# PEER layer: the expert activations of 64 tokens from gathered rows of u, the up products on 320 columns

## Chip, cores and metric

The kernel runs on one core of one Trainium2 chip. The metric is the device time of one execution in microseconds (us). The core has a matrix engine (PE, with its weight loads shown apart as PEld), a vector engine (DVE), a scalar engine (ACT), a general engine (POOL) and a queue engine (SP) that only issues DMAs; ACT and POOL issue DMAs too.

## What is computed

Two transformer blocks on 512 tokens of width 1024. The change lies in the last layer, a feed-forward layer that picks experts by product keys (PEER):

```
s = einsum('thpc,hpnc->thpn', q, subkeys)          # 8 heads, 2 halves, 128 keys each
s_top, i_top = top_k(s, 16)                        # of each half
best, pos = top_k(all 16 x 16 sums, 16)            # per head, so 128 experts per token
gates = softmax(best)
act = gelu(einsum('cd,ced->ce', xb, u[eb])) * gates
y = einsum('ce,ced->cd', act, v[eb])
```

There are 16,384 experts, as 128 blocks j of 128. u and v have one row of 1024 numbers per expert. After it come the residual sum and a last norm.

## The kernel before

Everything is float32; a product of two float32 matrices is made as three products of split halves (function mm3, line 192), each 128x128 weights against up to 512 columns.

In the layer (function peer) the tokens are treated in two ways. For tokens 0 to 127 the chosen rows of u and v are gathered, one expert slot k at a time: a row of uv (8 KB, u beside v) per token by an indirect DMA on POOL (gather, line 1421), a dot with the token's row on DVE (line 1429) and a weighted sum (line 1438). For tokens 128 to 511 nothing is gathered. The activations of all experts are computed as dense products: for each block j, `up(j)` runs 8 chunks x 3 products with 384 columns (TD = 384, one per token). They are multiplied by a sparse gate matrix and go through `down`, 18 products of 512 columns per block with v.

The gate matrix comes from one-hot products. `route(t)` finds experts and gates of the 128 tokens of group t on DVE (top-16 searches, index arithmetic, three large one-hot steps per half). `transposed` brings them to columns. `onehots(t)` works in 32 steps of 4 tokens (here called quads): DVE or POOL build the one-hots oh1 (of the row key) and oh2 (of the column key, scaled by the gate), PE multiplies them (line 1344), ACT copies the 128x512 result into `stage` (line 1346). For t = 1 and 2 `stage` is written to DRAM (`Gd`, line 1356) and read back block by block later; for t = 3 it stays on the chip.

While DVE works on that, PE is given `fill`s: up products of the first NA = 42 blocks, made ahead (`up_store`), their gelu stored in DRAM (`Hd`). Weights of u and v come through SP's queue (`pump`, line 110, 512 KB each), ACT makes the high half (line 115), and POOL or DVE the low half (line 118), as the list `lsplit` says. There are three buffers for loaded tiles and three pairs for split ones in this part.

So the layer has two parts. In the first one, routing, one-hots and 42 fills, in the order: 6 fills, route 1, one-hots 1 (with 6 fills), write of Gd with 8 fills, route 2, one-hots 2, and so on. In the second one the 128 blocks run in the order `mix`: a block whose up is not yet made makes it (`gate`), the others read it back, then `down`; the 128 gathers of tokens 0 to 127 run beside it. A list scheduler orders each engine's instructions by the dependences; the engines then run them strictly in that order.

Of the kernel before, what the change touches and what calls it, by code (L numbers as in the profile page):

```python
# [26 lines left out]
NA = 42  # L27
FIRST, FLUSH = 6, (2, 2, 2, 2)
# [15 lines left out]
def body(tc, A, out, upto=None, dbg=None):  # L44
# [1109 lines left out]
    def peer(norm):  # L1154
        H, L = norm.h, norm.l
        TD = 384
# [8 lines left out]
        Hd = dram.tile([NA, P, TD], F32, name="Hd")  # L1165
        keep = ctx.enter_context(tc.tile_pool(name="keep", bufs=1, reuse_waits="tile"))
        xnh = keep.tile([P, 8, TD], F32R, name="xnh")
        xnl = keep.tile([P, 8, TD], F32R, name="xnl")
# [27 lines left out]
        for i in range(16):  # L1196
# [15 lines left out]
            if 0 < i < 9:  # L1212
                c = i - 1
                xf = axps()[:, :TD]
                V.scalar_tensor_tensor(xf, xT[:, c, P:], vec("ffn_norm2", c), norm.rstd[:, P:],
# [23 lines left out]
        def up_store(j):  # L1239
            ps = mmps()[:, :TD]  # L1240
            up(j, ps)
            g = hp.tile([P, TD], F32, name="gel", tag="gel", bufs=3)
            SC.activation(g, ps, AF.Gelu)
            nc.scalar.dma_start(Hd[j], g)
# [8 lines left out]
        def route(t):  # L1253
# [8 lines left out]
            for i0, n, w, o in ((0, 1, 16, 0), (1, 2, 8, 16), (3, 5, 4, 32), (8, 8, 1, 52)):  # L1262
# [4 lines left out]
                                .to_broadcast([P, 8, n, w]), ALU.add)  # L1267
            for h in range(8):
                top16(bv[:, h], bi[:, h], cd[:, h])
            pf = r_("pf", (P, 8, 16))  # L1270
            V.tensor_copy(pf, bi)
            fi, fj, w_ = (r_(n, (P, 8, 16)) for n in ("fi", "fj", "fw"))
            for n, (sh, off) in enumerate(((3, -1.0), (2, -5.0))):
# [5 lines left out]
                else:  # L1279
                    V.scalar_tensor_tensor(fi, w_, off, fi, op0=ALU.add, op1=ALU.max)  # L1280
            V.scalar_tensor_tensor(fi, pf, -44.0, fi, op0=ALU.add, op1=ALU.max)
            V.scalar_tensor_tensor(fj, fi, -16.0, pf, op0=ALU.mult, op1=ALU.add)
            for m, off in ((-8.0, -8.0), (-4.0, -20.0), (-1.0, -44.0)):
                V.scalar_tensor_tensor(w_, fi, m, pf, op0=ALU.mult, op1=ALU.add)
                V.scalar_tensor_tensor(fj, w_, off, fj, op0=ALU.add, op1=ALU.max)
            ev = []
            for half in range(2):
# [3 lines left out]
                                iotap.rearrange("p (o i) -> p o i", o=1).to_broadcast([P, P, 16]), ALU.is_equal)  # L1291
                o4 = oh.rearrange("p (h k) i -> p h k i", k=16)
                V.tensor_tensor(o4, o4, tf[:, :, half].rearrange("p h (o i) -> p h o i", o=1)
                                .to_broadcast([P, 8, 16, 16]), ALU.mult)
                e = r_(f"e{half}", (P, P), bufs=2)
                V.tensor_reduce(e, oh, axis=AX.X, op=ALU.add)
                ev.append(e)
            gt = gate0 if t == 0 else r_("gt", (P, P), bufs=2)
# [7 lines left out]
            return ev[0], ev[1], gt  # L1306
# [3 lines left out]
        def transposed(t):  # L1310
            pt = axps()
            for n, a in enumerate(route(t)):
                PE.transpose(pt[:, n * P:(n + 1) * P], a, ident)
            rt = b_("rt", (P, 3, P), bufs=3)
# [3 lines left out]
        def onehots(t, rt):  # L1318
            io4 = iotp.rearrange("p (o i) -> p o i", o=1).to_broadcast([P, 4, P])
            stage = [stp.tile([P, 64, P], F32, name="stage", tag="stage", bufs=2) for _ in range(2)]  # L1320
            for q4 in range(32):
                t4 = slice(4 * q4, 4 * q4 + 4)
# [4 lines left out]
                if q4 % 3 == 1:  # L1327
# [22 lines left out]
            if t == 3:  # L1350
                return stage
# [340 lines left out]
```

## Time and profile before

| | us |
|---|---|
| median of 3 runs | 2962.44 |
| lowest, highest | 2959.42, 2965.99 |
| the profiled execution, its own time | 2960.28 |
| its span | 2957.9 |
| PE busy | 2900.9 (98%) |
| DVE busy | 1929.8 (65%) |
| ACT busy | 1376.7 (47%) |
| POOL busy | 1158.4 (39%) |

The span runs from the first instruction to the last; the execution's own time holds 2.4 us around it. Busy PE is counted from a matmul's start to its modelled end, and matmuls overlap, so the distance from start to start tells what one costs. The layer's products with u begin at 1750 us of the span.

### The profile page before, as it was taken

The page shows a single profiled execution, that of the slowest core. Times are in us where ns is not written, and L with a number is a line of the kernel's source. Part 1 is how long each engine was busy: PE and PEld are TensorE (multiplying, and loading weights), DVE is VectorE, ACT ScalarE, POOL GpSimd, SP SyncE. Part 2 cuts the span into 40 slices and gives each one's busy share as a digit, 9 for nine tenths or more (in the row PEclk, how much of TensorE's full clock was granted, in tenths as well). Part 3 has the DMA queues.
Part 4 walks back from the last instruction along what each step waited for, and adds up shares of the span by engine and source line. Part 5 has one row for each costly group of instructions (what it writes and reads, how often), then busy time and mean ns, then how long its engine had stood idle before and what let it go on. Part 6 is the DMA issues. An engine that isn't in the chain of part 4 may idle for free.

```text
span 2957.9 us, 46911 instructions
## 1 busy us (share of the span) xinstructions
PE 2900.9 (98%) x18211; PEld 2619.5 (89%) x18211; DVE 1929.8 (65%) x3505; ACT 1376.7 (47%) x2346; POOL 1158.4 (39%) x749
## 2 busy tenths in 40 slices
PE   8999999999999999999999999889999999999998
PEld 8999999988899999776688888888889888888887
DVE  4556645567664646537655788888677776776676
ACT  4454433356542425434544447567444444444444
POOL 4224323342232424104421435446455554555453
PEclk9999999999999999999999999999999999999999
DMA  4112333331123223221142232773888888888885
GB/s 136 67 52 101 98 96 101 97 104 36 65 97 97 96 98 110 85 72 52 49 150 66 86 111 79 226 225 113 304 330 311 312 317 316 330 307 302 308 315 188
DMA packets 166126, 473.41 MB, mean 160 GB/s; under 512 B 15368, under 2 KB 79240, under 8 KB 149520
## 3 DMA queue, kind: packets, MB, share of 16 engines
q1 hardware_dynamic: 135840, 322.73, 32.4%
q0 software_dynamic: 18432, 134.23, 11.8%
q10 hardware_dynamic: 11632, 13.46, 1.4%
q8 instruction: 143, 2.34, 0.3%
q14 instruction: 79, 0.65, 0.1%
HBM read 443.23 MB, written 27.13 MB: 159 GB/s over the span
## 4 chain that ended last, share of the span: by engine, by line
PE 89%; DVE 4%; ACT 3%; DMA 2%; issue 2%; POOL 1%; SPq 0%; ACTq 0%; DVEq 0%; POOLq 0%
PE mm L192 65%; PE ax L192 16%; PE ax L1344 2%; DMA w<-in_pu_dram 1%; ACT wh L115 1%; ACT stage L1346 1%; PE mm L1027 1%; PE ax L478 1%; PE ax L1207 1%; PE ax L997 0%; PE ax L453 0%; DVE wl L118 0%; DVE oh L1342 0%; PE mm L1021 0%; DMA xT<-in_xT_dram 0%
## 5 line engine op out<-in xcount | busy, mean ns | idle before, releaser
L118 POOL TENSOR_TENSOR wl<-w,wh 128x1024 fp32r<-128x1024 f32 x242 | 618.5, 2556 | 1058.2 <-ACT wh L115 893.7
L115 ACT ACTIVATE wh<-w 128x1024 fp32r<-128x1024 f32 (+1 forms) x530 | 560.0, 1057 | 854.1 <-PE mm L192 484.9
L192 PE MATMUL mm<-sh,wh 128*128 128x256 f32 (+2 forms) x3144 | 747.7, 303 | 7.0 <-ACT sh L225 6.2
L192 PE MATMUL mm<-sl,wh 128*128 128x256 f32 (+2 forms) x3144 | 744.6, 302 | 1.8 <-POOL sl L205 1.6
L192 PE MATMUL mm<-sh,wl 128*128 128x256 f32 (+2 forms) x3144 | 743.1, 301 | 1.0 <-DVE wl L118 1.0
L118 DVE TENSOR_TENSOR wl<-w,wh 128x1024 fp32r<-128x1024 f32 (+1 forms) x288 | 367.9, 1277 | 284.1 <-ACT wh L115 275.7
L192 PEld LDWEIGHTS mm<-sh,wh 128*128 128x128 f32 (+1 forms) x3144 | 498.9, 188 | 40.1 <-ACT sh L225 6.2
L192 PEld LDWEIGHTS mm<-sl,wh 128*128 128x128 f32 (+1 forms) x3144 | 497.9, 188 | 31.8 <-POOL sl L205 2.0
L192 PEld LDWEIGHTS mm<-sh,wl 128*128 128x128 f32 (+1 forms) x3144 | 497.9, 188 | 30.1 <-DVE wl L118 1.3
L192 PE MATMUL mm<-xnh,wl 128*128 128x384 f32 x688 | 237.1, 345 | 4.5 <-POOL wl L118 3.9
L192 PE MATMUL mm<-xnh,wh 128*128 128x384 f32 x688 | 237.5, 345 | 4.0 <-ACT wh L115 3.9
L192 PE MATMUL mm<-xnl,wh 128*128 128x384 f32 x688 | 236.8, 344 | 0.0
L285 DVE TENSOR_TENSOR xT<-xT,mm 128x512 f32<-128x512 f32 x80 | 54.7, 686 | 163.4 <-PE mm L192 163.4
L192 PE MATMUL mm<-wh,al 128*128 128x512 f32 x384 | 150.1, 391 | 2.5 <-DVE al L1471 2.5
L192 PE MATMUL mm<-wh,ah 128*128 128x512 f32 x384 | 150.3, 391 | 1.7 <-ACT ah L1470 1.7
L192 PE MATMUL mm<-wl,ah 128*128 128x512 f32 x384 | 150.2, 391 | 0.0
L192 PE MATMUL ax<-wh,ah 128*128 128x512 f32 x384 | 149.8, 390 | 0.0
L192 PE MATMUL ax<-wl,ah 128*128 128x512 f32 x384 | 149.7, 390 | 0.0
L192 PE MATMUL ax<-wh,al 128*128 128x512 f32 x384 | 149.4, 389 | 0.0
L561 POOL TENSOR_TENSOR y<-y 128x512 f32<-128x512 f32 x44 | 56.9, 1293 | 220.7 <-ACT y L560 220.7
L553 DVE SCALAR_TENSOR_TENSOR y<-u,vecs,y 128x512 f32<-128x512 f32 x88 | 113.9, 1295 | 44.5 <-ACT y L552 44.5
L192 PEld LDWEIGHTS mm<-xnh,wh 128*128 128x128 f32 x688 | 131.3, 191 | 6.4 <-ACT wh L115 4.6
(465 smaller groups left out, 5434.7 us busy)
## 6 DMA issues: line engine op xcount, KB each, us to landing
w<-in_pu_dram SPq DMA_DIRECT2D x128, 512.0 KB
w<-in_pv_dram SPq DMA_DIRECT2D x128, 512.0 KB
w<-in_up_dram SPq DMA_DIRECT2D x88, 512.0 KB
w<-in_down_dram SPq DMA_DIRECT2D x48, 512.0 KB
Gd<-stage SPq DMA_DIRECT2D x16, 1024.0 KB
gm<-Gd SPq DMA_DIRECT2D x128, 128.0 KB
w<-in_pq_dram SPq DMA_DIRECT2D x16, 512.0 KB
Hd<-gel ACTq DMA_DIRECT2D x42, 192.0 KB
```

What stands on the lines that cost most here:

```text
L115: SC.activation(h[:, :n], w[:, :n], AF.Copy)
L118: ins = eng.tensor_tensor(l[:, :n], w[:, :n], h[:, :n].bitcast(F32), ALU.subtract)
L192: PE.matmul(ps[:, c:c + w], lhsT=a, rhs=b[:, c:c + w], start=start and c == 0 and a is lh and b is rh, stop=stop and c + w == n and a is ll)
L285: V.tensor_tensor(xT[:, c], xT[:, c], ps, ALU.add)
L478: PE.matmul(ps[:, s], lhsT=a, rhs=b, start=i == 0, stop=i == len(mms) - 1)
L553: V.scalar_tensor_tensor(y, u[:, 0:S], w[0], y, op0=ALU.mult, op1=ALU.add)
L561: G.tensor_tensor(val, val, gate, ALU.mult)
L1027: PE.matmul(po[e * 64:e * 64 + 64, c * P:], lhsT=vs[:, c, hd * 64:hd * 64 + 64], rhs=at[:, c * P:], start=c == 0, stop=c == 3)
L1207: PE.matmul(pss[:, t * P:(t + 1) * P], lhsT=q[:, t * P:(t + 1) * P], rhs=sk, start=True, stop=True)
L1344: PE.matmul(pg[:, k * P:(k + 1) * P], lhsT=oh1[:, k], rhs=oh2[:, k], start=True, stop=True)
L1346: SC.activation(stage[jh][:, :, t4].rearrange("p j t -> p t j"), pg.rearrange("p (t j) -> p t j", t=4)[:, :, jh * 64:jh * 64 + 64], AF.Copy)
```

## The change

Tokens 128 to 191 (64 of them) get their activations from gathered rows too, but only u is gathered, and the result goes into the gate matrix: the gate of each chosen expert is multiplied by gelu(u . x) before the one-hots are built, so that what the one-hot products spread is the finished activation. The up products then need the columns of tokens 192 to 511 alone: 320 in place of 384. The down products stay as they are.

64 tokens x 128 experts are laid out as 128 partitions x 64 slots. `udots_begin` makes the indices and the tokens' rows (small products with the identity) and starts two gathers; `udots` has 64 steps, a dot on DVE in place over a gathered tile of 128 rows of 4 KB, and the gather for two steps later on POOL. The gathered tiles take turns in three buffers that lie in xT; xT is therefore first copied to DRAM (`Xd`) and read back later for the residual. `udots_end` applies gelu and multiplies the gates.

`route` and `udots` are now generators whose steps are issued between the quads of another group. The order is: 14 fills and route 2; one-hots of group 2 with route 1, `udots_begin` and route 3 between its quads and 20 fills; one-hots of group 3 with the 64 dots between and 20 fills; one-hots of group 1 with route 0 between and 12 fills. NA is 66. All low halves of weights are made on POOL in this part (`lsplit` = [G]; before, DVE and POOL took turns outside the one-hots). POOL builds oh1 in 8 of 32 quads instead of 11. For oh2, every second quad is one comparison of 512 columns into PSUM and one multiplication on DVE, in place of four small operations. `stage` holds the whole group as 2 halves of 64 tokens; each half of groups 2 and 3 is written to Gd as soon as its 16 quads are done, in rows of 64 numbers (256 bytes) where there were 128 (512 bytes). The residual is now added after the first down product. The core of the diff:

```diff
-NA = 42
-FIRST, FLUSH = 6, (2, 2, 2, 2)
+NA = 66
+FIRST = 14
-        TD = 384
+        TD, TU, HT = 384, 320, 64
+        Xd = dram.tile([P, 8, S], F32, name="Xd")
+        for c in range(0, 8, 4):
+            nc.scalar.dma_start(Xd[:, c:c + 4], xT[:, c:c + 4])
...
+        def ugather(k):
+            G.indirect_dma_start(out=ub[k % 3], out_offset=None, in_=urows,
+                                 in_offset=bass.IndirectOffsetOnAxis(ap=idx1[:, k:k + 1], axis=0))
...
+        def udots():
+            for k in range(HT):
+                u = ub[k % 3]
+                V.scalar_tensor_tensor(u, u, 1.0, xn1, op0=ALU.mult, op1=ALU.mult, accum_out=dval[:, k:k + 1])
+                if k + 2 < HT:
+                    ugather(k + 2)
+                yield 1.4
+
+        def udots_end(res):
+            SC.activation(dval, dval, AF.Gelu, scale=rdup[:, 0:1])
+            rt = transposed(res)
...
+            V.tensor_tensor(rt[:, 2, 0:HT], rt[:, 2, 0:HT], pv[:, 0:HT], ALU.mult)
+            return rt
-                if q4 % 3 == 1:
+                if q4 % 4 == 1:
...
+                if q4 % 2 == 0:
+                    own = V.tensor_tensor(oh2, cols(1), io4, ALU.is_equal)
+                    for k in range(4):
+                        SC.activation(oh2[:, k], oh2[:, k], AF.Copy, scale=rt[:, 2, 4 * q4 + k:4 * q4 + k + 1])
+                else:
+                    eq = mmps().rearrange("p (t j) -> p t j", t=4)
+                    V.tensor_tensor(eq, cols(1), io4, ALU.is_equal)
+                    own = V.tensor_tensor(oh2, eq, cols(2), ALU.mult)
...
+                if q4 % 16 == 15 and t > 1:
+                    c0 = (t - 2) * P + (q4 // 16) * HT
+                    for j0 in range(0, P, 16):
+                        nc.sync.dma_start(Gd[j0:j0 + 16, :, c0:c0 + HT].rearrange("j i t -> i j t"),
+                                          st[:, j0:j0 + 16])
...
-        lsplit[:] = [V, G]
+        lsplit[:] = [G]
         fill(FIRST)
-        for t in (1, 2, 3):
-            rt = transposed(t)
-            lsplit[:] = [G]
-            stage = onehots(t, rt)
+        res = []
+        for _ in route(2, res):
+            pass
+        onehots(2, transposed(res), between2(), 3.1, 20)
+        onehots(3, rts[0], between3(), 2.9, 20)
+        onehots(1, rts[1], route(0, r0), 1.45, 12)
         fill(NA)
...
-                up(j, g)
-                SC.activation(g, g, AF.Gelu)
+                up(j, g[:, HT:])
+                SC.activation(g[:, HT:], g[:, HT:], AF.Gelu)
             else:
-                SC.activation(g, st, AF.Copy)
-            V.tensor_tensor(g[:, :2 * P], g[:, :2 * P], gm, ALU.mult)
-            V.tensor_tensor(g[:, 2 * P:], g[:, 2 * P:], stage[j // 64][:, j % 64], ALU.mult)
+                SC.activation(g[:, HT:], gs, AF.Copy)
+            SC.activation(g[:, :HT], stage[:, 0, j], AF.Copy)
+            V.tensor_tensor(g[:, HT:P], g[:, HT:P], stage[:, 1, j], ALU.mult)
+            V.tensor_tensor(g[:, P:], g[:, P:], gm, ALU.mult)
```

POOL's instructions, before, in the middle of the one-hots of group 2. `wl` is the low half of a weight tile, made from the loaded tile `w` and its high half `wh`; `oh` is oh1 of a quad:

```order
L1329 TENSOR_SCALAR oh_19337<-iot,rt 128x128 x4
L118 TENSOR_TENSOR wl<-w,wh 128x1024 x2
L1329 TENSOR_SCALAR oh_19417<-iot,rt 128x128 x4
L1329 TENSOR_SCALAR oh_19497<-iot,rt 128x128 x4
L118 TENSOR_TENSOR wl<-w,wh 128x1024
L1329 TENSOR_SCALAR oh_19543<-iot,rt 128x128 x4
L118 TENSOR_TENSOR wl<-w,wh 128x1024
```

And POOL's, now, in the middle of the one-hots of group 3 (L1347 is the gather of one slot, L1403 oh1):

```order
L1403 TENSOR_SCALAR oh_20403<-iot,rt 128x128 x4
L1347 DMA xT<-in_uv_dram,idx_17832 128x1024 x2
L118 TENSOR_TENSOR wl<-w,wh 128x1024
L1347 DMA xT<-in_uv_dram,idx_17832 128x1024 x3
L118 TENSOR_TENSOR wl<-w,wh 128x1024
L1347 DMA xT<-in_uv_dram,idx_17832 128x1024 x3
L118 TENSOR_TENSOR wl<-w,wh 128x1024
L1403 TENSOR_SCALAR oh_20576<-iot,rt 128x128 x4
```

Two or three gathers now stand between two low halves of weights, so a low half, and the up product that needs it, comes behind gathers that wait for a buffer.

DVE's instructions, now, at the same place (L1374 is a dot, L1405 and L1408 are oh1 and oh2, L1413 and L1414 the comparison and the multiplication for oh2):

```order
L1374 SCALAR_TENSOR_TENSOR xT,dval<-xT 128x1024 x2
L1405 TENSOR_TENSOR oh_20385<-rt,ax 128x512
L1408 TENSOR_TENSOR oh_20387<-rt,ax 128x512
L1374 SCALAR_TENSOR_TENSOR xT,dval<-xT 128x1024
L1413 TENSOR_TENSOR mm<-rt,ax 128x512
L1374 SCALAR_TENSOR_TENSOR xT,dval<-xT 128x1024
L1414 TENSOR_TENSOR oh_20408<-mm,rt 128x512
L1374 SCALAR_TENSOR_TENSOR xT,dval<-xT 128x1024 x2
```

Each one-hot has one or two dots ahead of it, and waits when such a dot waits for its rows.

SP's queue, now, around the first two half groups written to Gd (before, two writes of 1 MB stood between one or two loads):

```order
L110 DMA w<-in_pu_dram 128x1024 x20
L1433 DMA Gd<-stage 128x16x64
L110 DMA w<-in_pu_dram 128x1024
L1433 DMA Gd<-stage 128x16x64 x7
L110 DMA w<-in_pu_dram 128x1024 x9
L1433 DMA Gd<-stage 128x16x64
L110 DMA w<-in_pu_dram 128x1024
L1433 DMA Gd<-stage 128x16x64 x7
```

Seven writes of 512 KB now follow each other before the next load of weights.

## Rows read from the trace of the kernel before

**Rows 1.** Windows: PE, PEld, DVE, ACT, POOL busy, PE clock, DMA share, GB/s.
```profile
core 0: us, PE busy (x) PEld busy (x) DVE busy (x) ACT busy (x) POOL busy (x), PEclk, DMA share, GB/s
1750.00:1792.00 42.00, 36.12 (x202) 35.56 (x201) 40.59 (x163) 17.16 (x24) 12.52 (x5) 0.92 0.38 131
1792.00:1848.00 56.00, 54.81 (x389) 52.23 (x387) 47.63 (x117) 49.31 (x115) 35.53 (x48) 1.00 0.21 69
1848.00:1886.00 38.00, 32.15 (x168) 30.63 (x167) 31.54 (x100) 13.95 (x22) 7.91 (x4) 0.87 0.96 286
...
2048.00:2072.00 24.00, 19.54 (x134) 18.45 (x134) 19.76 (x16) 10.18 (x19) 10.57 (x6) 1.00 0.55 184
2100.00:2900.00 800.00, 799.30 (x3957) 715.47 (x3956) 582.04 (x805) 350.67 (x666) 427.21 (x217) 1.00 0.85 313
```

**Rows 2.** PE in order of time: start, length; one up, one down, the last products.
```profile
2123.51 0.34 PE L192 MATMUL ax<-xnh,wh 128*128 128x384 f32 x1
...
2127.67 0.39 PE L192 MATMUL mm<-wh,ah 128*128 128x512 f32 x1
...
2131.76 0.39 PE L192 MATMUL mm<-wh,ah 128*128 128x512 f32 x1
...
2946.44 4.17 PE ax L192 x18
```

**Rows 3.** PE in an earlier feed-forward layer, products of 256 columns.
```profile
300.09 0.39 PE L192 MATMUL mm<-sh,wl 128*128 128x256 f32 x2
...
302.81 0.39 PE L192 MATMUL mm<-sh,wl 128*128 128x256 f32 x2
```

**Rows 4.** PE, one-hot products of two quads (two records each).
```profile
1815.74 2.12 PE L1344 MATMUL ax<-oh,oh 128*128 128x128 f32 x16 [0.33 <-ACT oh L1340]
```

**Rows 5.** DVE in order of time: route 1 first to last, then one-hots.
```profile
1758.15 0.41 DVE L1254 CAST ax<-ti 128x256 f32<-128x256 uint32 x1
...
1773.63 2.50 DVE L1285 SCALAR_TENSOR_TENSOR fj<-fw,fj 128x128 f32<-128x128 f32 x1
...
1787.69 2.27 DVE L1296 TENSOR_REDUCE e<-oh 128x128 f32<-128x2048 f32 x1
...
1793.02 0.68 DVE L1335 TENSOR_TENSOR oh<-rt,ax 128x512 f32<-128x512 f32 x1
1793.62 1.36 DVE L1342 TENSOR_SCALAR oh<-ax,rt 128x128 f32<-128x128 f32 x4
```

**Rows 6.** POOL in order of time: oh1, two gathers in a row, a gather, a low half.
```profile
1817.95 2.35 POOL L1329 TENSOR_SCALAR oh<-iot,rt 128x128 f32<-128x128 f32 x4 [2.38 <-PE ax L1344]
...
2070.84 0.94 POOL L1421 DMA_INDIRECT xT<-in_uv_dram,idx  x1 [0.30 <-issue]
2072.08 0.93 POOL L1421 DMA_INDIRECT uv<-in_uv_dram,idx  x1 [0.30 <-issue]
...
2402.98 1.69 POOL L1421 DMA_INDIRECT uv<-in_uv_dram,idx  x1 [2.56 <-DVE xt L1438]
...
2407.01 2.42 POOL L118 TENSOR_TENSOR wl<-w,wh 128x1024 fp32r<-128x1024 f32 x1
```

**Rows 7.** DVE in order of time, beside the last two rows of POOL.
```profile
2402.63 1.21 DVE L1429 SCALAR_TENSOR_TENSOR scr<-xT,xn 128x1024 f32<-128x1024 f32 x1
...
2403.78 1.28 DVE L1438 SCALAR_TENSOR_TENSOR xt<-xT,dot,xt 128x1024 f32<-128x1024 f32 x1
...
2408.62 1.90 DVE L1429 SCALAR_TENSOR_TENSOR scr<-uv,xn 128x1024 f32<-128x1024 f32 x1
```

**Rows 8.** ACT's queue issues a 512 KB load; DVE waits for its landing.
```profile
2064.20 0.34 ACTq L1383 DMA_DIRECT2D scr<-in_ffn_norm_row_dram  x1
...
2068.44 1.28 DVE L1407 SCALAR_TENSOR_TENSOR xn<-xt,prcol,scr 128x1024 f32<-128x1024 f32 x1 [2.13 <-DMA scr<-in_ffn_norm_row_dram]
```

**Rows 9.** SP's queue: the first write to Gd, the last weight load between.
```profile
1851.67 4.05 SPq L1356 DMA_DIRECT2D Gd<-stage  x2
...
1886.34 3.52 SPq L110 DMA_DIRECT2D w<-in_pu_dram  x1
```

More of the change, by code (lines that the diff above doesn't have):

```diff
@@ L1251, in fill, with route @@
                     up_store(ahead.popleft())
-        def route(t):
+        def route(t, out):
             V.tensor_copy(tfp.rearrange("p (a b) -> p a b", b=16), ti[t])
@@ L1305, in route, with transposed @@
             V.tensor_tensor(g3, g3, sm.rearrange("p (h o) -> p h o", o=1).to_broadcast([P, 8, 16]), ALU.mult)
-            return ev[0], ev[1], gt
+            out.extend((ev[0], ev[1], gt))
+            yield 2.0
         stp = rctx.enter_context(tc.tile_pool(name="st", bufs=1, side="right", reuse_waits="tile"))
-        def transposed(t):
+        stage = stp.tile([P, 2, P, HT], F32, name="stage")
+        def transposed(res):
             pt = axps()
-            for n, a in enumerate(route(t)):
+            for n, a in enumerate(res):
@@ new lines, in udots @@
+        def udots():
[8 more added lines that the diff above has]
+            rt = transposed(res)
+            pv = axps()
+            for n in range(2):
+                PE.matmul(pv[n * HT:(n + 1) * HT, 0:HT], lhsT=dval, rhs=ident[:, n * HT:(n + 1) * HT],
+                          start=True, stop=True)
+            V.tensor_tensor(rt[:, 2, 0:HT], rt[:, 2, 0:HT], pv[:, 0:HT], ALU.mult)
+            return rt
@@ L1319, in onehots @@
+        def onehots(t, rt, steps, pace, fills):
             io4 = iotp.rearrange("p (o i) -> p o i", o=1).to_broadcast([P, 4, P])
-            stage = [stp.tile([P, 64, P], F32, name="stage", tag="stage", bufs=2) for _ in range(2)]
+            spent, filled = 0.0, 0
             for q4 in range(32):
+                st = stage[:, q4 // 16]
                 t4 = slice(4 * q4, 4 * q4 + 4)
@@ L1360, in peer @@
[L1360 to L1365 removed]
+                    PE.matmul(pg[:, k * P:(k + 1) * P], lhsT=oh1[:, k], rhs=oh2[:, k], start=True, stop=True)
+                o = 4 * (q4 % 16)
+                SC.activation(st[:, :, o:o + 4].rearrange("p j t -> p t j"),
+                              pg.rearrange("p (t j) -> p t j", t=4), AF.Copy)
+                with tc.issue_after(own.ins):
+                    while spent < pace * (q4 + 1):
+                        c = next(steps, None)
+                        if c is None:
+                            break
+                        spent += c
@@ new lines, in onehots @@
+                n = fills * (q4 + 1) // 32
+                fill(n - filled)
+                filled = n
+                if q4 % 16 == 15 and t > 1:
[3 more added lines that the diff above has]
+                                          st[:, j0:j0 + 16])
+            for _ in steps:
+                pass
+        r1, r0, rts = [], [], []
```

134 lines of the change are left out of this document (82 added, 52 removed).

## The prediction

> **What bounds the kernel now.** I read the windows first [rows 1]. From 2100 to 2900 us, the part of the 128 blocks, PE is busy 799.3 of 800 us with DVE at 582, POOL at 427 and the DMA share at 0.85 (313 GB/s): PE is the bound and little waits. Before that it is less even. The 42 us before the first one-hots hold 36.1 us of PE, the one-hots of group 1 (56 us) are PE-bound at 54.8, with DVE already at 47.6, and the 38 us in which the group is written to DRAM hold 32.2, with a DMA share of 0.96. These three stretches come three times, and 2048 to 2072 holds 4.5 us more of idle PE. Then I read single instructions in order of time for what one of each costs. The layer's products run from 1750 to the end of the last ones, 2946.44 + 4.17 = 2950.6 us [rows 2]: 1200.6 us. The sum below replaces this piece.
>
> What PE does there: an up product takes 2127.67 - 2123.51 = 4.16 us for 24 products, so 173.3 ns each, and a down 4.09 us for 18, so 227 ns [rows 2]. Two quads of one-hot products took 2.12 us to the modelled end of the last, which overlaps what follows; I take 0.98 us a quad [rows 4]. 128 x 4.16 + 128 x 4.09 + 96 x 0.98 = 532 + 524 + 94 = 1150 us. The other 50 are waits, half clock (0.92 and 0.87 granted in the uneven stretches [rows 1]), transposes and the residual.
>
> **What the change saves.** 320 columns do not occur before. 256 columns take (302.81 - 300.09)/24 = 113.3 ns [rows 3], 384 take 173.3; the middle is 143.3, and 173.3 less 64 columns at 2.4 GHz (26.7) is 146.6. I take 145.5: an up costs 3.49 us. 3072 products x 27.8 ns = **85 us less** (82 to 92). Downs and one-hot products stay.
>
> **What it adds, by stage.** The work for the 64 tokens lies in the first part, so I lay that part out again, each stage as long as its slowest engine, from 1750.
>
> Prices. DVE: route 1 ran from 1758.15 to 1787.69 + 2.27, 31.8 us [rows 5]; two low halves (2.4) go to POOL, and some 3.4 us were waiting like that of the 2.50 us operation on 128x128 [rows 5]: 25.5. One one-hot of 512 columns starts 0.60 after the one before [rows 5]; a quad has two of these and three quarters of a scalar part, and I take 43 us a group. A dot of 128x1024 takes 1.15 us from start to start (1.21 in the row) [rows 7]. POOL: a low half 2.4, oh1 of a quad 2.35, a gather 0.94 with 1.24 from start to start [rows 6].
>
> - Lead: 14 fills x 3.49 = 49 us of PE. Route 2 (8 + 25.5 + the transposes) is done before that. **50**.
> - Group 2: PE 20 x 3.49 + 32 x 0.98 + 5 for small products = 106; DVE 43 + two routes 51 + 2 for the indices = 96, and waits on POOL, priced next, of some 14: 110. Two engines that feed each other in a strict order: **116**.
> - Group 3 with the dots: PE 101; DVE 43 + 64 x 1.15 = 117; POOL 20 x 2.4 + 8 x 2.35 + 64 x 1.24 = 48 + 19 + 79 = 146. So POOL becomes the bound, for the first time in this layer.
> - Group 1: PE 12 x 3.49 + 31 = 73; DVE 43 + 25.5 + 8 of waits = 76: **80**.
>
> For group 3 the engines also hold each other. POOL's low half of 2407.01 ran 2.42 us, and DVE's dot of 2408.62, which began in it, took 1.90 [rows 6, 7]. POOL's gather of 2402.98 took 1.69, to 0.83 after the end of the dot of 2402.63, while the weighted sum of 2403.78 ran 1.28 beside that gather [rows 6, 7]. So a gather waits at its start for a running dot, and a dot is not held by a gather. In this stage some twenty low halves and eight oh1 meet a DVE that is seldom idle, and each costs one of the two about half an operation, 0.6 us, and most gathers 0.4: 146 + 28 x 0.6 + some 10 = 172.
> The second limit of this stage is the ring of three tiles. The next gather into a tile is queued when its dot is done: dot 1.15, POOL's queue ahead of it about 1.2 (two or three gathers, or a low half), transfer about 4.2 to 5.1 (a load of the same 512 KB, issued at 2064.20, was waited for until 2068.44 [rows 8]; gather and its generation are longer by up to 0.94), 0.6 to be seen: 7.2 to 8.1 us for three dots, or 64 x 2.4 to 2.7 = 154 to 173. Both limits come out near 170: **168**, from 146 (POOL with no waits) to 205 (both limits in turn, one fifth more). Behind a dot that waits stands the one-hot of the next quad on DVE, and behind that PE's product; the fills need POOL's low halves, which stand behind gathers that wait for a tile. So PE stands there 168 - 101 = 67 us.
>
> First part: 50 + 116 + 168 + 80 = 414 us, to 2164. PE's work in it is 66 x 3.49 + 94 + 5 = 329.
>
> Second part: 62 x 3.49 + 128 x 4.09 = 216 + 524 = 740 us, with 6 for the residual and copies, 8 for the start (4.5 in the window from 2048 [rows 1], and now the reload of xT, the stored activations and the first gathers together), and 8 for weights that come late: **762**.
>
> Sum 414 + 762 = 1176 against 1200.6: **24.6 us less**. The profiled execution took 2960.28, so 2935.7; the median shown is 2.2 above it: **2938**.
>
> **What costs nothing, and what hides it.** The copy of xT to DRAM (2 MB, 6.7 us at 313 GB/s) runs beside the query products ahead of 1750, on ACT's queue. If it were late it would hold the first dots, 100 us on. Its reload stands beside the last fills; unhidden it would be 6.7 us in the start's 8. The copy of 64 columns per block on ACT, some 0.27, has room beside PE's 5.8 us a block. The larger NA only moves fills to where PE would wait.
>
> Writing `stage` to DRAM: before, 8 MB went out between 1851.67 and 1886.34 with five loads of weights between [rows 9], a stretch at a share of 0.96 [rows 1]; less the loads, some 25 us for 16,384 pieces of 512 bytes. Now a half is 4 MB in 16,384 pieces of 256: 12 us if bytes count, 25 if pieces count, 50 if a short piece costs double. SP holds the next loads behind it, but six tiles (three loaded, three split) cover 35 us at 5.8 a fill in group 2, 50 and 40 in the next two. I take 25, hidden.
>
> The Trainium skill, "DMA: Bandwidth & Descriptors", section Specifications, gives 512 bytes as the least transfer at line rate and a read-modify-write below it. That speaks against this change; no row of the trace before has 256-byte writes. By that rule the 50 us would hold, which is the slower rival below.
>
> **Rivals.**
> 1. *More gain.* POOL's pauses fall in DVE's, transfers overlap: group 3 takes 146, group 2 takes 111, and weights are never late (8). 35 us more: about **2902**. For it: PE had 799.3 of 800 in the steady part [rows 1]. Against it: DVE in group 3 runs in strict order, so its waits don't fall where they suit.
> 2. *DMA bounds the second part.* A block with an up moves 1994 KB now and 2071 before, but PE would take 5.78 us per block (the mean over 128) in place of 6.89. 313 GB/s at 0.85 would become 353 at 0.96. If the queues give no more than 0.92, 339 GB/s, a block takes 6.02, the part 770 and not 740: 30 us, 8 of which I have counted: **2960**, no change. For it: 0.96 was reached only while PE had pauses (32.2 of 38) [rows 1].
> 3. *Slower: short pieces starve the weights.* The place is SP's queue after each half of groups 2 and 3. If a 256-byte piece costs over 1.4 times one of 512, the write outlasts the 35 us of tiles. At double: 50 us each, PE in group 2 short by 15, in group 1 by 10, and the gathers, which share the queues' engines, slower by some 25 in group 3: 50 in all, **2988**. For it: a share of 0.96 at only 286 GB/s with 512-byte pieces [rows 1], where loads in long rows got 313 at 0.85. Against it: that the price of a piece doubles when it halves.
> 4. *Slower: gather and dot exclude each other throughout.* Then POOL and DVE take turns in group 3: 146 + 64 x 1.15 = 220, 52 more: **2990**. The row of 1.28 us beside a gather speaks against it [rows 7], the gather of 1.69 for it [rows 6].
>
> The Trainium skill, "SBUF — State Buffer", section "SBUF: two separate sides", says that an operation of DVE with two SBUF inputs and one of POOL share a port pair that is locked for the whole instruction, the loser fully blocked. That is rival 4 in full; the trace agrees for the low half (1.90 us) and for the gather's start, and not for the operation of 1.28 us.
>
> A smaller one inside the range: PE is busy only 60% in group 3, and its clock was 0.87 where it was busy 85% [rows 1]. If it got 1.2 GHz throughout, its work would be 101 x 2 = 202, 34 over 168.
>
> **How the numbers follow.** Forecast 0.46 (2938; of its own 2918 to 2955), rival 1 0.20, rival 2 0.12, rival 3 0.13, rival 4 0.09. 0.2% is about what a measurement of this kernel can tell from no change. Faster is the forecast and rival 1, 0.66; same is rival 2, 0.12; slower is 3 and 4, 0.22. The range holds the forecast, rival 2 and most of the others: 2895 (POOL's floor and the largest saving) to 2988.
>
> **What would show it.** A 320-column product of 143 to 147 ns. The last dot of group 3 about 330 us after 1750, POOL near 90% busy in that stage, PE near 60%; a stage of 146 means rival 1, over 200 rivals 3 or 4. In the second part PE still full at a DMA share of 0.93 to 0.97; if PE waits for `w` there, rival 2. A half's writes to DRAM ending within 30 us of their start; if 50, with PE waiting for `wl` or `w` behind, rival 3. A dot of over 1.6 us beside a gather, rival 4. The forecast is wrong if the ring turns in other than 7 to 8 us for three dots, or if the granted clock in group 3 is near 0.5.

## The result and the profile after

The changed kernel takes 2988.38 us (median of 4 runs, 2987.53 to 2992.23) against 2960.93 before; the ratio is 1.0087, its 95% interval 1.0066 to 1.0107. It is 27 us slower where 25 us faster was forecast. The profiled execution took 2987.53, its span 2985.8.

The windows of the changed kernel, cut at the stages of the prediction (columns as in [rows 1]; the last one is a piece of the second part):

```profile
1750.00:1802.00 52.00, 50.87 (x348) 50.37 (x346) 34.54 (x137) 26.23 (x38) 34.07 (x15) 1.00 0.58 182
1802.00:1921.00 119.00, 104.58 (x724) 100.63 (x725) 102.64 (x266) 79.83 (x137) 64.49 (x53) 0.94 0.55 161
1921.00:2129.00 208.00, 143.76 (x786) 132.46 (x785) 149.87 (x201) 84.17 (x143) 155.90 (x119) 0.83 0.85 268
2129.00:2217.00 88.00, 80.51 (x584) 77.19 (x584) 69.01 (x169) 70.79 (x128) 44.88 (x40) 1.00 0.57 162
...
2300.00:2900.00 600.00, 594.53 (x3009) 514.88 (x3008) 504.85 (x698) 307.30 (x668) 328.26 (x181) 1.00 0.94 354
```

| stage | forecast, us | measured, us |
|---|---|---|
| lead, 14 fills | 50 | 52 |
| one-hots of group 2 | 116 | 119 |
| one-hots of group 3, with the dots | 168 | **208** |
| one-hots of group 1 | 80 | 88 |
| second part, to the last product at 2979.1 | 762 | 762 |
| sum | 1176 | 1229 |

53 us are missing, and 40 of them lie in the stage with the dots. The reader should look there at what no engine does: PE, DVE and POOL are busy 144, 150 and 156 of 208 us, so none is full, and the DMA share is 0.85, under the 0.94 that the second part sustains at 354 GB/s.

The up products cost what was forecast. PE in the changed kernel, two products with 28 others between them:

```profile
2004.24 0.31 PE L192 MATMUL mm<-xnh,wh 128*128 128x320 f32 x1
...
2008.49 0.30 PE L192 MATMUL mm<-xnh,wl 128*128 128x320 f32 x1
```

4.25 us for 29 steps are 146.6 ns a product (forecast 145.5, before 173.3), so the 64 columns give 3072 x 26.7 ns = 82 us. They were given back in the stage with the dots.

What DVE does from the first dot (1922) to the last (2128) says how. Groups of instructions on DVE, with busy time, mean ns, and the idle time before them with its releaser (L1374 the dots, the others the one-hots), and POOL's groups in the same window:

```profile
L1374 DVE SCALAR_TENSOR_TENSOR xT<-xT 128x1024 f32<-128x1024 f32 x64 | 107.0, 1680 | 57.8 <-DMA xT<-in_uv_dram,idx 57.6
L1405 DVE TENSOR_TENSOR oh<-rt,ax 128x512 f32<-128x512 f32 x23 | 15.6, 677 | 0.0
L1413 DVE TENSOR_TENSOR mm<-rt,ax 128x512 f32<-128x512 f32 x16 | 11.0, 686 | 0.0
L1414 DVE TENSOR_TENSOR oh<-mm,rt 128x512 f32<-128x512 f32 x16 | 10.9, 683 | 0.3
L1408 DVE TENSOR_TENSOR oh<-rt,ax 128x512 f32<-128x512 f32 x16 | 10.9, 679 | 0.0
```

```profile
L1347 POOL DMA_INDIRECT xT<-in_uv_dram,idx x61 | 68.8, 1127 | 50.3 <-DVE xT L1374 41.8 <-issue 6.7 <-PE mm L192 0.8
L118 POOL TENSOR_TENSOR wl<-w,wh 128x1024 fp32r<-128x1024 f32 x22 | 53.0, 2410 | 0.5
L1403 POOL TENSOR_SCALAR oh<-iot,rt 128x128 f32<-128x128 f32 x35 | 33.8, 976 | 0.5 <-ACT rt L1331 0.3
```

Nearly every idle microsecond of DVE stands before a dot that waits for its rows; the one-hots wait for nothing (0.3 us in all). So on DVE the 206 us from the first dot to the last are a sum: one-hots 43 (by their pitch of 0.60, [rows 5]), dots 64 x 1.15 = 74, 29 more because the mean dot is 1.68 long where one that nothing holds is 1.22, and 58 of waiting for rows: 204 us. On POOL the same time is 156 of work and 50 of waits, 42 of these for dots. Each of the two engines waits for the other: a gather for the dot that frees its tile, a dot for the rows of its gather.

The 29 us are a lock with POOL: a dot that meets a low half there stands until the low half has ended. DVE and POOL in order of time:

```profile
2003.22 1.21 DVE L1374 SCALAR_TENSOR_TENSOR xT<-xT 128x1024 f32<-128x1024 f32 x1
...
2007.78 3.34 DVE L1374 SCALAR_TENSOR_TENSOR xT<-xT 128x1024 f32<-128x1024 f32 x1 [1.59 <-DMA xT<-in_uv_dram,idx]
2011.05 0.08 DVE L1374 DVE_READ_ACCUMULATOR xT<-xT 128x1 f32 x1
2011.05 1.22 DVE L1374 SCALAR_TENSOR_TENSOR xT<-xT 128x1024 f32<-128x1024 f32 x1
```

```profile
2002.97 0.95 POOL L1347 DMA_INDIRECT xT<-in_uv_dram,idx  x1 [1.37 <-DVE xT L1374]
...
2007.66 2.37 POOL L118 TENSOR_TENSOR wl<-w,wh 128x1024 fp32r<-128x1024 f32 x1
2010.00 2.67 POOL L1403 TENSOR_SCALAR oh<-iot,rt 128x128 f32<-128x128 f32 x1
```

The dot of 2003.22 stands beside a gather and is not held. The dot of 2007.78 begins 0.12 us after a low half and takes 3.34: 2.2 until the low half ends and 1.1 for itself. In the whole stage 17 of the 64 dots begin within a low half and take 2.73 us on average; the 24 that meet nothing but gathers take 1.22. Then POOL's next operation, a quarter of oh1 of 0.59 in [rows 6], takes 2.67 beside the two dots. The Trainium skill, "SBUF — State Buffer", section "SBUF: two separate sides", says that such a pair holds each other for the whole instruction; the rows of low half and dot agree.

### The profile page after: what moved, and what is told of

Same layout as the page of the kernel before. It is cut to its first block, busy times and chain, and to the rows that moved or that the text cites. A ratio compares the mean times of both kernels' runs of the same rounds, so it can differ in the third digit from the quotient of the medians.

```text
span 2985.8 us, 47379 instructions
## 1 busy us (share of the span) xinstructions
PE 2857.4 (96%) x18255; PEld 2561.3 (86%) x18255; DVE 2006.1 (67%) x3484; ACT 1430.8 (48%) x2464; POOL 1244.9 (42%) x800
## 4 chain that ended last, share of the span: by engine, by line
PE 77%; DVE 6%; issue 5%; POOL 5%; ACT 3%; DMA 3%; SPq 0%; ACTq 0%; DVEq 0%; POOLq 0%
PE mm L192 60%; PE ax L192 11%; POOL wl L118 2%; POOL xT L1347 2%; PE ax L1417 1%; DMA xT<-in_uv_dram,idx 1%; DVE scr L1530 1%; ACT wh L115 1%; POOL oh L1403 1%; DVE xt L1539 1%; PE mm L1027 1%; PE ax L1211 1%; DMA w<-in_pv_dram 1%; DVE xT L1374 0%; PE ax L997 0%
## 5 line engine op out<-in xcount | busy, mean ns | idle before, releaser
L118 POOL TENSOR_TENSOR wl<-w,wh 128x1024 fp32r<-128x1024 f32 x265 | 665.0, 2511 | 956.3 <-ACT wh L115 769.7
L118 DVE TENSOR_TENSOR wl<-w,wh 128x1024 fp32r<-128x1024 f32 (+1 forms) x265 | 339.4, 1281 | 234.0 <-ACT wh L115 228.5
L192 PE MATMUL mm<-xnh,wh 128*128 128x320 f32 x784 | 256.3, 327 | 2.0 <-ACT wh L115 2.0
L192 PE MATMUL mm<-xnh,wl 128*128 128x320 f32 x784 | 252.0, 321 | 3.0 <-POOL wl L118 3.0
L192 PE MATMUL mm<-xnl,wh 128*128 128x320 f32 x784 | 252.9, 323 | 0.0
L1417 PE MATMUL ax<-oh,oh 128*128 128x128 f32 x768 | 130.9, 308 | 80.9 <-ACT oh L1410 42.8
L1417 PEld LDWEIGHTS ax<-oh,oh 128*128 128x128 f32 x768 | 112.3, 208 | 98.0 <-ACT oh L1410 52.0
L192 PEld LDWEIGHTS mm<-xnh,wl 128*128 128x128 f32 x784 | 155.1, 198 | 3.6 <-POOL wl L118 3.5
L192 PEld LDWEIGHTS mm<-xnl,wh 128*128 128x128 f32 x784 | 155.4, 198 | 1.3
L1419 ACT ACTIVATE stage<-ax 128x512 f32<-128x512 f32 x96 | 103.5, 1094 | 108.8 <-PE ax L1417 108.3
```

The source lines that it names most:

```text
L118: ins = eng.tensor_tensor(l[:, :n], w[:, :n], h[:, :n].bitcast(F32), ALU.subtract)
L192: PE.matmul(ps[:, c:c + w], lhsT=a, rhs=b[:, c:c + w], start=start and c == 0 and a is lh and b is rh, stop=stop and c + w == n and a is ll)
L1417: PE.matmul(pg[:, k * P:(k + 1) * P], lhsT=oh1[:, k], rhs=oh2[:, k], start=True, stop=True)
L1419: SC.activation(st[:, :, o:o + 4].rearrange("p j t -> p t j"), pg.rearrange("p (t j) -> p t j", t=4), AF.Copy)
```

## The experiments

Turn times below are means over the dots, from the end of a dot to the start of the gather that refills its tile, to the landing, to the dot there, to its end: in the changed kernel 1.74 + 6.03 + 0.30 + 1.70 = 9.8 us for three dots (64 x 9.8 / 3 = 209). "Dots" is the time from the first dot to the end of the last.

**No gathers.**

```diff
-                V.scalar_tensor_tensor(u, u, 1.0, xn1, op0=ALU.mult, op1=ALU.mult, accum_out=dval[:, k:k + 1])
-                if k + 2 < HT:
-                    ugather(k + 2)
+                V.scalar_tensor_tensor(u, u, 0.0, xn1, op0=ALU.mult, op1=ALU.mult, accum_out=dval[:, k:k + 1])
```

> The first two gathers of u rows stay, the other 62 are left out, and the 64 dots run over rows that are already there (the activations of tokens 128 to 191 are not those of the reference). In the changed kernel the dots take 206 us from the first's start to the last's end, 3.25 us each, and three dots in a row take 9.78: dot 1.70, from its end to the start of the gather that refills the tile 1.74, gather 1.13, its landing 4.90, and 0.30 to the next dot. Theory (the ring of three tiles sets the stage): without gathers DVE is the longest engine with 43 + 64 x 1.15 = 117 us and some waits on low halves of weights, so the dots take about 130 us and the kernel some 75 us less, about 2913. Rival A (dots and POOL's low halves hold each other, and the strict order of DVE does the rest): the dots still take over 165 us, 2945 or more. Rival B (the 256-byte writes to DRAM starve the fills): PE still waits there, over 165 us too, with PE waiting for wl or w.

2936.85 us, 52 less than the changed kernel. The window of the dots, and DVE's dots in it:

```profile
1923.00:2068.00 145.00, 119.30 (x749) 113.46 (x747) 145.00 (x195) 81.96 (x135) 93.76 (x53) 0.91 0.60 158
```

```profile
L1374 DVE SCALAR_TENSOR_TENSOR xT<-xT 128x1024 f32<-128x1024 f32 x64 | 106.6, 1701 | 0.0
```

Between both expectations: the waits for rows are gone and the stage is 61 us shorter, the held dots are as long as before (1701 ns), and DVE is busy 145.0 of 145.0 us. So the waits for rows and the lock are two terms of one sum, on DVE; 145 is what remains without the first, 28 more than its own work of 117.

**Four tiles in the ring.**

```diff
-        xn1, ub = flat[:, 0:D], [flat[:, (n + 1) * D:(n + 2) * D] for n in range(3)]
+        xn1, ub = r_("xn1", (P, D)), [flat[:, n * D:(n + 1) * D] for n in range(4)]
...
-                if k + 2 < HT:
-                    ugather(k + 2)
+                if k + 3 < HT:
+                    ugather(k + 3)
...
```

> Four tiles in the ring of gathered u rows in place of three (the scaled token rows move to a tile of their own), gathers three dots ahead. Theory (ring): the same 9.78 us now serve four dots, 2.45 each, 156 us for the dots, 50 less; POOL's own work of 146 us with some waits is then as long, so 155 to 170, and the kernel 36 to 50 us less: 2940 to 2952. Rival A (locks between dots and low halves): no tile more changes those; under 15 us less, 2973 or more. Rival C (gathers limited by the DMA engines, which the writes and weights share): landing grows with one more in flight, to 8 us, and under 15 us are won.

2978.70 us, 10 less; the dots take 190. The theory missed: the waits for rows fell from 58 to 39 us only, and the 10 us are what rivals A and C said (under 15). DVE's dots:

```profile
L1374 DVE SCALAR_TENSOR_TENSOR xT<-xT,xn 128x1024 f32<-128x1024 f32 x64 | 110.8, 1746 | 39.4 <-DMA xT<-in_uv_dram,idx 39.1
```

The turn did not stay at 9.8: it took 12.1 us for four dots, 3.0 until the gather starts (1.74 before), 7.4 from there to the dot (6.3 before) and 1.7 for the dot. Three dots were 3.3 us each, four are 3.0.

**Low halves on DVE in this stage.**

```diff
+        lsplit[:] = [V]
         onehots(3, rts[0], between3(), 2.9, 20)
+        lsplit[:] = [G]
```

> During the one-hots of group 3 the low halves of weights are made by DVE in place of POOL. POOL loses some 22 x 2.4 = 53 us, DVE gets 22 x 1.28 = 28. Theory (ring): dots are no longer held by a low half on POOL (1.70 goes to 1.2) and gathers no longer stand behind one (1.74 to about 1.2): a turn of 8.7 us, 186 us, 20 less, about 2968; DVE's 117 + 28 = 145 stay under that. Rival A (locks set the stage): all excess of the dots (33.6 us over 64) and of the waiting low halves goes: 50 us less, 2938. Rival D (DVE is the bound with its waits): longer, over 2995.

2988.27 us (2980.80 to 2999.26 in 6 runs), no change; in the profile, which is of the fastest of these, the dots take 194, 12 less. DVE's dots and low halves:

```profile
L1374 DVE SCALAR_TENSOR_TENSOR xT<-xT 128x1024 f32<-128x1024 f32 x64 | 77.7, 1226 | 56.4 <-DMA xT<-in_uv_dram,idx 56.1
L118 DVE TENSOR_TENSOR wl<-w,wh 128x1024 fp32r<-128x1024 f32 x18 | 22.0, 1221 | 0.9 <-ACT wh L115 0.9
```

The lock is gone (1226 ns a dot) and its cause is shown. But for the 29 us of lock DVE took over 22 us of low halves, and the waits for rows did not move. POOL's busy time fell from 156 to 101 us here, so POOL's load is not what sets the stage.

**Long pieces to DRAM.**

```diff
-                    c0 = (t - 2) * P + (q4 // 16) * HT
+                    c0 = 64 * (t - 2) + 32 * (q4 // 16)
...
-                        nc.sync.dma_start(Gd[j0:j0 + 16, :, c0:c0 + HT].rearrange("j i t -> i j t"),
-                                          st[:, j0:j0 + 16])
+                        gj = c0 + j0 // 4
+                        nc.sync.dma_start(Gd[gj:gj + 4].rearrange("j (i a) t -> (j i) (a t)", a=4),
+                                          st[:, j0:j0 + 16].rearrange("p j t -> p (j t)"))
```

> The writes of the gate matrix to DRAM keep their number, place and bytes, but go in pieces of 4 KB in place of 256 bytes (so the values come to other places of the matrix than the reference wants). Theory (ring): a gather lands after 6.0 us where the second part's first estimate was 4.2 to 5.1; writes that share the DMA engines are part of that, about half the stage's time. With them 4 KB long, landing is about 0.7 us shorter on average, a turn 9.1, the dots 194 us: 12 less, and as the 256-byte writes are otherwise hidden, 2976. Rival B (short pieces starve the weights, the slower rival of the prediction): 30 to 50 us less, 2940 to 2958, with the stage of group 2 and of group 1 shorter too. If nothing under 5 us changes, short pieces cost nothing here.

2999.08 us of two runs (2993.37, 3004.79), not faster; its profiled execution was 11 us later by 800 us already and 14 by 1300, where the two programs do the same. The dots take 206 us as before, at a share of 0.79 in place of 0.85:

```profile
1935.00:2141.00 206.00, 140.42 (x769) 129.24 (x767) 143.79 (x198) 82.91 (x141) 155.40 (x117) 0.82 0.79 271
```

The 256-byte pieces cost the DMA engines some 0.06 x 206 = 12 us in this stage, and their length costs the kernel nothing that two runs show. The Trainium skill, "DMA: Bandwidth & Descriptors", section Specifications, names 512 bytes as the least transfer at line rate; the share agrees, and no wait hung on it here. The packets in the traces give the price: one of 256 bytes held an engine for 18 ns in this stage of the changed kernel, one of 512 for 27 ns while the kernel before wrote to Gd. So a piece of half the length costs two thirds, and neither the doubling of rival 3 nor its 1.4 times came.

**No dots.** udots_begin, the dots and the gathers left out.

```diff
-            udots_begin(r1)
-            yield 3.0
...
-            yield from udots()
-            rts.append(udots_end(r1))
+            rts.append(transposed(r1))
+            yield 1.0
```

> The 64 gathers and dots, and the indices and token rows for them, are left out; the rest of the change stays, the 320 columns and the new order too (so the activations of tokens 128 to 191 are left out of the result). What the dots cost, in the changed kernel as a whole: the stage of group 3 should fall to PE's 106 us from 208, and the kernel by about 100 us to 2886; against the kernel before that is the 85 us that 64 columns are worth less what the rest of the change costs or gives. If the stage stays over 130 us without any dot, the one-hots, low halves and writes hold it by themselves, and the ring theory is only part of it.

2896.27 us: 65 less than the kernel before (ratio 0.9778, 0.9756 to 0.9801) and 92 less than the changed one. The stage of group 3 takes 113 us, PE busy 105:

```profile
1930.00:2043.00 113.00, 105.28 (x746) 104.39 (x745) 48.37 (x79) 77.55 (x139) 66.81 (x53) 0.95 0.75 198
```

So the 320 columns with all else are worth 65 us, and the dots cost 92. They break even with the kernel before at a stage some 27 us shorter than 208. The other 17 of the 82 us go to the rest of the change; where was not followed up.

**Four tiles, and low halves on DVE.** The edits of the second and third run together.

> Four tiles in the ring (as in the run with a ring of four) and, in the stage of group 3, the low halves on DVE (as in that run). Each alone left the other limit: with four tiles the dots took 189 us with POOL busy 157 of them and dots 38 us longer by locks; with low halves on DVE 194 us, at a turn of 9.2 us for three tiles. Theory (two limits next to each other, the ring at three tiles and POOL's and DVE's exclusive work): together a turn of 9.2 to 9.6 us serves four dots, 2.35 each, 150 us; DVE has 117 + 28 = 145. So the dots take 155 to 165 us and the kernel 40 to 50 us less than the changed one: 2938 to 2948, faster than the kernel before. Rival C (DMA engines limit the gathers): not under 180 us, 2965 or more.

2970.85 us (10 runs), ratio to before 1.0030 (1.0020 to 1.0040): 18 less than the changed kernel, still slower than before. The dots take 181, not 155 to 165. DVE is busy 137 of these 181 us, 23 of them with low halves; it waits 40 for rows and 4 for a high half.

**No fills beside the dots.** FIRST = 34, and no fills in the one-hots of group 3.

> The 20 fills of the stage of group 3 are made in the lead (34 there in place of 14), so the stage of the dots has no loads of weights, no low halves and no up products; it costs 70 us of PE in the lead, where nothing hides. In question is whether a gather's 6.0 us from start to landing is its own or comes of what shares the DMA engines. Theory (own): landing stays at 5.5 to 6, dots 1.3, the turn 8.5, the dots take 180 us, the kernel 3030. Rival C (shared engines): landing falls to 4.8 like the first gather of the row, the turn is under 7.5 and the dots take 155 to 160, the kernel 3005.

3034.45 us, and 177 us for the dots: the forecast of the theory, 3030 and 180, and not that of shared engines. With 3 loads of weights and 3 low halves at the stage's start in place of 22 each, and with hardly any up product, at a PE clock of 0.54, DVE still waits 59 us for rows:

```profile
L1374 DVE SCALAR_TENSOR_TENSOR xT<-xT 128x1024 f32<-128x1024 f32 x64 | 79.0, 1239 | 58.7 <-DMA xT<-in_uv_dram,idx 58.6
```

From the start of a gather to the dot in its tile it took 5.95 us, where it was 6.33 in the changed kernel. By the packets, a gather's last one ends 5.4 us after the gather's start here and 5.5 there (the landing is signalled some 0.5 us later). So the landing does not come of the loads of weights (their share of it is 0.1 to 0.4 us). Writes and other gathers still ran beside it, at a DMA share of 0.79; in the run without gathers the first two, with no others behind them, ended 5.0 us after their start. The turn of 8.5 us for three dots gives 64 x 8.5 / 3 = 181, and the stage without the lock is 29 us shorter than 206, as long as the lock was.

**Four tiles, low halves on DVE, long pieces.** The three edits together.

> The run with four tiles and low halves on DVE, whose dots took 181 us and not the 155 to 165 expected, at a DMA share of 0.92; here its writes to DRAM also go in pieces of 4 KB (values to other places of the matrix than the reference wants). With three tiles the long pieces took 0.06 of share off the stage (14 us of the engines' time) and nothing off the dots. Theory (with ring and locks out of the way the DMA engines are the next limit): the dots lose those 14 us, 165 to 169, and the kernel some 13 us, about 2958. Rival (the strict order on DVE and the chain of one-hots keep the 181): the dots stay within 4 us of 181 and the share falls to 0.86.

2972.19 us; the dots take 181 again, at a share of 0.86 in place of 0.92. The theory fell: the DMA engines are not the next limit. The wait for a high half is gone (4 us before), and the waits for rows are 44 us in place of 40.

**Five tiles, low halves on DVE.**

```diff
-        xn1, ub = r_("xn1", (P, D)), [flat[:, n * D:(n + 1) * D] for n in range(4)]
+        xn1, ub = r_("xn1", (P, D)), [flat[:, n * D:(n + 1) * D] for n in range(4)] + [r_("ua", (P, D))]
...
-                if k + 3 < HT:
-                    ugather(k + 3)
+                if k + 4 < HT:
+                    ugather(k + 4)
...
```

> The run with four tiles and low halves on DVE (dots 181 us, four dots in 11.4 us: 2.2 from a dot's end to the next gather into its tile, 8.1 from there to the next dot there, 1.2 the dot) with a fifth tile. That run and the one with long writes left the 181 us without an owner: not the locks (5 us over 64 dots), not the writes. Theory (the ring still, since DVE's bursts of one-hots and low halves and POOL's bursts of gathers don't overlap): a fifth tile gives 165 to 172 us, and the waits of dots for their rows fall from 40 us to 20. Rival (DVE with its 153 us and POOL in strict order): under 4 us are won.

2979.62 us in 8 runs (2967.05 to 2983.78, the profile being of the fastest); the dots take 181, nothing won: the rival's number. But the waits of dots for rows did fall, to 28 us, and another took their place. DVE's waits, SP's queue ahead of one of them, and that wait on DVE:

```profile
DVE xT L1374 <- DMA xT<-in_uv_dram,idx: 19.2, 8, 5.0
DVE wl L118 <- ACT wh L115: 16.7, 3, 8.9
DVE ua L1374 <- DMA ua<-in_uv_dram,idx: 8.5, 3, 3.8
```

```profile
1935.48 32.98 SPq L1433 DMA_DIRECT2D Gd<-stage  x7
1968.55 16.43 SPq L110 DMA_DIRECT2D w<-in_pu_dram  x6
```

```profile
1978.74 1.23 DVE L118 TENSOR_TENSOR wl<-w,wh 128x1024 fp32r<-128x1024 f32 x1 [7.25 <-ACT wh L115]
```

Seven writes of a half group take 33 us to issue on SP's queue (25 in the changed kernel, 31 with four tiles and low halves on DVE), with more gathers in flight beside them; the loads behind are late, so ACT's high half is late, and DVE's low half stands in the strict order ahead of the next dots. That is the place the prediction's rival 3 named, with 17 us of waits in this kernel; that the shortness of the pieces does it is not shown. The gathers land later too: the last packet ends 6.2 us after a gather's start here, 6.0 with four tiles and 5.5 in the changed kernel. In all three kernels with more than three tiles and low halves on DVE, DVE waits 44 us in the stage (40 + 4, 44 + 0, 28 + 17), and the dots take 181. What sets these 181 us stays open.

**The dots spread over two stages.** Routes 2 and 1 in the lead (18 fills), two dots after each step of route 3 in the one-hots of group 2, the rest so with route 0 in those of group 3; four tiles; oh1 on POOL for group 1 alone.

```diff
...
+            for c in route(3, res):
+                yield c
+                yield next(dots)
+                yield next(dots)
...
+            for c in route(0, r0):
+                yield c
+                for _ in range(2):
+                    yield next(dots, 0.0)
+            yield from dots
...
+        for _ in route(1, r1):
+            pass
+        onehots(2, rt2, between2(), 2.75, 20)
+        onehots(3, rts[0], between3(), 2.3, 20)
+        onehots(1, rts[1], iter(()), 1.45, 8)
...
```

> The same work spread over the stages: routes 2 and 1 in the lead (18 fills), the 64 dots in both the stage of group 2 (with route 3) and that of group 3 (with route 0), four tiles in the ring, oh1 on POOL only for group 1; low halves on POOL as in the changed kernel. If POOL and DVE are the limits and no longer the ring, each of the two stages has DVE 45 + 37 + 26 = 108, POOL 50 + 40 = 90, PE 106, and with 20 us of waits each takes 125 to 130; lead 64, last stage 58: 375 us for the first part in place of 467, the kernel about 2890 to 2905. If the ring or the landing of the gathers were the limit still, 32 dots x 3 = 96 us would hide under these stages, so nothing of it would be seen. If lock waits grow with the overlap of POOL's low halves and DVE (both busy all the time), the two stages take 150 each and the kernel 2940.

2939.24 us (2937.13 to 2942.39): ratio to the kernel before 0.9921 (0.9904 to 0.9938), 49 us less than the changed kernel. It beats both. Windows of its first part, and its dots on DVE:

```profile
1750.00:1821.00 71.00, 69.31 (x473) 67.67 (x471) 67.45 (x251) 35.12 (x49) 45.04 (x19) 1.00 0.59 185
1821.00:1966.00 145.00, 113.51 (x750) 107.85 (x751) 135.51 (x250) 82.63 (x136) 92.83 (x59) 0.93 0.84 265
1966.00:2099.00 133.00, 111.57 (x737) 107.03 (x736) 126.06 (x232) 81.24 (x140) 79.42 (x44) 0.90 0.90 267
2099.00:2171.00 72.00, 67.26 (x494) 63.46 (x493) 45.57 (x74) 64.23 (x122) 39.94 (x41) 1.00 0.63 172
```

```profile
L1374 DVE SCALAR_TENSOR_TENSOR xT<-xT,xn 128x1024 f32<-128x1024 f32 x64 | 104.2, 1636 | 2.3 <-DMA xT<-in_uv_dram,idx 2.3
```

The waits for rows are gone (2.3 us): other work of DVE stands between the dots while rows land, with four tiles in the ring. The locks stay (1636 ns). The two stages came to 145 and 133 and not to 125 to 130: DVE is busy 135.5 and 126.1 in them, where the expectation had 108 of work and 20 of waits.

**The spread kernel with three tiles.** The ring of the changed kernel in it.

> The spread version with three tiles in the ring of u rows in place of four. A turn of 9.8 us for three dots, as in the changed kernel, is 3.27 each, 36 dots in the first of its two stages 118 us and 28 in the second 92, under the 145 and 133 that these stages take. Theory (a ring under other work costs nothing): 2939, within 8 us. Rival (the ring's waits stand on DVE in strict order and add up): 15 to 30 us more, 2955 to 2970.

2940.80 us, within 2 us of four tiles: the theory's number. The same ring that left DVE 58 us idle leaves it 19 us idle when the dots are spread over two stages, and the time does not show these. So in the spread kernel waits on DVE do not add to the time one for one, as they do in the stage of the dots; why was not followed up.

**The spread kernel with all scaling of oh2 on ACT** for groups 2 and 3.

```diff
-                if q4 % 2 == 0:
+                if q4 % 2 == 0 or t > 1:
```

> The spread version (2939 us), in whose two stages with dots DVE is busy 135.5 of 145 and 126.1 of 133 us, with the oh2 of every quad of groups 2 and 3 scaled by ACT (busy 82 in each of them) in place of every second by a DVE multiplication. 16 multiplications of 0.68 us less per stage on DVE, 16 x 4 x 0.39 = 25 us more on ACT. If DVE sets these stages: 2 x 11 = 22 us less, about 2918. If the DMA engines set them (share 0.84 and 0.90): under 5 us. If ACT with its copies in a strict order becomes late: same or slower.

2936.39 us (2929.28 to 2949.15 in 4 runs), ratio to before 0.9903 (0.9872 to 0.9934): not told apart from the spread kernel. The two stages of its profiled execution:

```profile
1835.00:1974.00 139.00, 117.15 (x782) 109.87 (x781) 128.33 (x232) 98.38 (x201) 97.42 (x59) 0.93 0.90 284
1978.00:2105.00 127.00, 106.80 (x670) 101.91 (x669) 116.55 (x214) 94.24 (x197) 69.67 (x43) 0.88 0.86 262
```

From the first to the last one-hot product they take 138 and 127 us, where they took 144 and 129, so 8 of the 22 us. DVE lost 14 us of work in them and gained 6 of waits. Which of its waits took these wasn't followed up.

## Why the prediction was wrong

- **The saving** was right: 82 us for the columns, 146.6 ns a product (85 and 145.5 forecast). Two slips beside it changed nothing: 31.8 less 2.4 and 3.4 is 26.0 for a route, not 25.5; and rival 2's 1994 and 2071 KB are the means over all 128 blocks by the sizes of their tiles, not those of a block with an up.
- **Lead, group 2, group 1 and the second part** were within 8 us each. PE has 594.5 of 600 us at a DMA share of 0.94 (forecast 0.93 to 0.97), so rival 2 did not come, though its share did. That the second part is 762 to the microsecond is in part luck: its 8 us were for weights that come late, and PE never waited for weights there; it waited 9.4 us for ACT's high half of the activations, and 0.7 for the reload of xT.
- **The stage of the dots** is the step that failed, 208 for 168. The text took it as the larger of two limits that "come out near 170", POOL's queue with half an operation per meeting, and the ring at 7.2 to 8.1 us a turn, and kept the two apart. POOL's queue was not it: with 53 us less work on POOL the dots take 194. The ring was, but at a turn of 9.8 us, the text's own sign of being wrong; and the lock that it had priced on POOL's queue lengthens this turn. DVE, with its floor of 117, was looked at and set aside, since POOL's 146 was more. But both limits make DVE wait, and DVE runs one strict order: in this stage the held dots (29 us) and the late rows (58 us) are added to its 117. The run without gathers shows the first kind alone (145 us, 28 over 117), the run without fills the second alone (177 us, 60 over 117); 117 + 28 + 60 = 205, and the changed kernel has 206.
- **Two prices in it** were too low. In the turn of the ring the dot took 1.70 for 1.15, POOL's queue 1.74 for 1.2, and the landing 6.0 for 4.2 to 5.1 taken from a plain load; the run without fills shows that the loads of weights are not the reason. And a low half cost the dot that met it all that was left of the low half, 1.5 us on average over 17 dots and up to 2.2 for one low half, not half an operation, 0.6. The row behind that price had it: the dot of 1.90 us ended 1.1 after the low half [rows 6, 7].
- **The rivals.** Rival 3 named 2988, which is the time, by another mechanism, so that is chance: long pieces in place of short ones won nothing. Late weights behind the writes cost DVE more than 4 us only in the kernel with five tiles (17). Rival 4 named 2990, and is out too: the dot beside a gather takes 1.22, and the lock comes from low halves and, for less, oh1. The stage of both was "over 200", and is; what fills it is the lock with low halves and the waits for rows together.
- **The break-even** was in the numbers: the forecast gain of 25 us hung on a stage of 168, and its own upper end of 205, "both limits in turn", would have given 2975, slower than before. That case is near what came, and the sum went without it.

## What to carry to other kernels

For a stage in which engines feed each other in a strict order, add up on each engine its own work, the time others hold it and the time its inputs come late; the largest of the plain sums is a floor, not a forecast. A ring of buffers that is short by a few microseconds a turn was mended here by placing its consumer among other work of the same engine (58 us of waits became 19, and 2 with one buffer more) sooner than by more buffers alone (58 became 39 with one more). Moving work away from an engine that holds another one gains little if the engine that takes it is the one that was held: DVE took back 22 of the 29 us.

## What the runs showed of the hardware

- A gather of 128 rows of 4 KB took some 6 us from its start on POOL to its landing, and 5.95 to the dot when few loads but writes and other gathers ran beside it. With more gathers in flight its last packet came later: 5.5 us after its start with three tiles, 5.9 with four, 6.2 with five and low halves on DVE.
- A gather on POOL does not hold a dot on DVE (1.22 us for 24 dots that met only gathers), though a gather that starts in a running dot takes 1.66 us in place of 0.95. A low half on POOL holds a dot until it ends (3.34 us for a dot that began 0.12 after it), and dots hold oh1 on POOL (2.67 us for an operation of 0.59).
- A piece of 256 bytes written to DRAM held a DMA engine for 18 ns, one of 512 bytes for 27.
- The DMA engines carried 354 GB/s at a share of 0.94 over 600 us with PE still busy 594.5 of them.
